# Moving a 31-tap convolution onto VectorE, reordering a mixer's projections, and placing input sums behind evacuations

## The chip, the core and the metric

The kernel runs on one core of a Trainium2 chip. The time is that of one execution on the device, in microseconds (us); three executions of the kernel before were timed. TensorE is called PE, VectorE DVE, ScalarE ACT, GpSimd POOL and SyncE SP, as in the profile.

## The reference, cut to what matters

A trunk of two layers runs over 512 latent tokens (stream x) and 256 context tokens (stream c) of 1024 channels, all in fp32. Each layer is

```
h += 1/2 * gate1 * SwiGLU(mod(RMSNorm(h)))     # FFN, 2816 hidden channels
h +=       gate2 * Mixer(mod(RMSNorm(h)))
h += 1/2 * gate3 * SwiGLU(mod(RMSNorm(h)))
```

The four FFNs are called the first to the fourth (FFN0 to FFN3 in the code's tables). The mixer of layer 0 is a convolution beside a bidirectional gated DeltaNet (GDN); that of layer 1 is a state-space model (S5):

```
h    = a * sigmoid(g)                          # 512 channels, glu of the projection
conv = silu(layer_norm(depthwise31(h) + conv_b))       # 31 taps a channel
qkv  = silu(depthwise5(qkv_raw)); q, k = l2norm(q), l2norm(k)   # 4 heads of 128
y    = concat([conv, gdn(q, k, v, a, beta) * silu(gate)]) @ w_out
```

## The kernel before

**Products.** Activations lie with channels on partitions. Every fp32 product is three fp32r matmuls of high and low parts (L381, L383, L385). A weight tile `raw` comes by DMA on SP; ACT copies its high part `whi` (L163) and DVE, or POOL, subtracts for `wlo` (L164).

**FFN.** The 2816 hidden channels are 22 units of 128. A direct unit is `ua`, `ub` products over 8 row blocks; its evacuation `evac` is silu on ACT, multiply on DVE, high part on ACT, low part on DVE. `NDIR` says how many units of each FFN are direct; the rest are fast units (`up_fast`): seven products of half size, which need sums of the inputs (`fast_sums`, k = 0 to 3, on DVE with two splits on ACT and DVE) and sums of the weights (on POOL). The lists `FP0` to `FP3` say at which point of the FFN each of the four sums is issued: (1, 4) in the middle of the first units' context products, "b2" ahead of unit 2's products, a plain 2 behind unit 2's evacuation. After some units a down projection (`down`, `both`) writes banks d0x, d1x, d0c and so on, and `resid` (L701) adds them to `hT`.

**Second FFN and the S5 build.** While the second FFN runs, a generator `build` makes the matrices of the S5 mixer on DVE, POOL and PE. `with_bg` advances it by `NBG` yields after each step.

**Mixer of layer 0, projections (616 to 872 us).** `MIXORD` lists the steps: a0 the decay inputs, q0 to q5 the projections of two channel blocks each (q0, q1 are q heads, q2, q3 are k heads, q4, q5 are v), g0, g1 the gates, u2, u3 the glu of convolution blocks 2 and 3, k0 to k3 the transposes of a k head to tokens, s0 to s2 small scalar stages. After a q step's products the 5-tap convolution runs (ACT L961, then four DVE operations L963 for each of two blocks), then silu (L969). In the next step, behind its products, `held_back` issues the squares on ACT (L982), which PE sums over channels into `sqn` (L985); L986 takes them to `nrm`. For v the transposes `tt` are copied to `ts` with the factor RINV (L1003).

**Convolution.** `conv31(m, ...)` is a generator, one tap or so a yield. Blocks m = 0, 1 run during the projections: POOL does 10 taps (L862 multiply, L863 add), DVE 21 (L867, L870) and one addition. `conv_taps(n)` issues n yields at the end of a step, by the table `TAPS`. Blocks 2, 3 run beside the GDN: `side_work` loads `hb` from DRAM by SP, then ACT multiplies 16 taps (L873, tile ctt), POOL adds them (L874, tile cvp), DVE does 15 (L870, tile cvs) and an addition (L884).

**GDN (872 to about 1170 us).** `run` goes round its generators (scans, the levels of a triangular inverse, the preparation of the next chunk) and advances each by one yield a round, then `side_work` by one. A level is PE w (L1269), ACT copy (L1270), PE b (L1280), DVE update (L1283); L1231, L1241, L1244, L1250 and L1251 prepare a chunk on DVE or POOL. Each engine works off its instructions in the order of issue.

Of the kernel before, what the change touches and what calls it, by code (L numbers as in the profile page):

```python
# [9 lines left out]
F32 = mybir.dt.float32  # L10
# [4 lines left out]
ALU = mybir.AluOpType  # L15
# [20 lines left out]
TAPU = 8  # L36
# [4 lines left out]
NBG = 5  # L41
S5RD = 3
TSTAT = 1
NDIR = (3, 16, 3, 3)
FP0 = [(1, 4), (1, 7), "b2", 2]
FP1 = [13, 14, "b15", 15]
FP2 = [(1, 4), (1, 7), "b2", 2]
FP3 = [(1, 4), (1, 7), "b2", 2]
# [4 lines left out]
MIXORD = "a0 q0 q1 q2 q3 s0 g0 s1 k0 g1 s2 k1 q4 k2 k3 q5 u2 u3"  # L53
TAPS = (10, 16, 4, 11)
# [5 lines left out]
def trunk_kernel(  # L60
# [468 lines left out]
    def ffn_steps(l, fi, zf, zt, nxt, parts=PARTS, rest=None, fast=0, prep=(), delay=False):  # L529
# [194 lines left out]
        def down(c0, nk, lastpart):  # L724
# [4 lines left out]
            def both(q):  # L729
                def fn(w):  # L730
                    for i in range(0, per, 2):
# [79 lines left out]
    NPOOL, NPOOL2 = TAPS[:2]  # L811
# [15 lines left out]
    def open_mixer():  # L827
# [16 lines left out]
        T["cp"] = p.tile([P, CW], F32, name="cp")  # L844
        T["ct"] = p.tile([P, CW], F32, name="ct")
# [5 lines left out]
    def conv31(m, hb, ca, cp, ct):  # L851

        w = lambda j: cwT[:, j * 4 + m:j * 4 + m + 1]
        n = NPOOL if ct is not None else NPOOL2
        pj = list(range(31 - n, 31))
        cps = cp if isinstance(cp, list) else [(cp, 0, CW)]
        for c_, a, b in cps:
            GP.tensor_scalar(c_, hb[:, pj[0] + a:pj[0] + b], w(pj[0]), par[:, CONVB_O + m:CONVB_O + m + 1], ALU.mult, ALU.add)
        k = 1
        while ct is not None and k < n:  # L860
            for c_, a, b in cps:
                GP.tensor_scalar(ct[:, a:b], hb[:, pj[k] + a:pj[k] + b], w(pj[k]), None, ALU.mult)  # L862
                GP.tensor_tensor(c_, c_, ct[:, a:b], ALU.add)  # L863
            k += 1
        if ct is not None:
            yield
        V.tensor_scalar(ca, hb[:, 0:CW], w(0), None, ALU.mult)  # L867
        yield
        for j in range(1, 31 - n):
            V.scalar_tensor_tensor(ca, hb[:, j:j + CW], w(j), ca, ALU.mult, ALU.add)  # L870
            while k < n and k * (31 - n) < j * n:
                t = tmp.tile([P, SAW], F32, tag="sa", name="ctt")
                SC.activation(t, hb[:, pj[k]:pj[k] + CW], AF.Copy, scale=w(pj[k]))  # L873
                GP.tensor_tensor(cp, cp, t, ALU.add)  # L874
                k += 1
            yield
        while k < n:
            t = tmp.tile([P, SAW], F32, tag="sa", name="ctt")
# [4 lines left out]
        for c_, a, b in cps:  # L883
            V.tensor_tensor(ca[:, a:b], ca[:, a:b], c_, ALU.add)  # L884
# [1417 lines left out]
```

## Time and profile before

| | us |
|---|---|
| three executions, median (lowest to highest) | 2963.92 (2960.92 to 2970.04) |
| the profiled execution | 2967.29 |
| its span | 2965.0 |
| busy PE / DVE / POOL / ACT | 2790.9 / 2066.2 / 1098.0 / 1090.2 |

PE is busy for 94% of the span. The rest is some 170 us of idle stretches, and there are stretches in which PE works at the lower of its clock's two levels (1.2 against 2.4 GHz); a granted clock of 1.00 in a row is the higher level throughout, 0.50 the lower. The page's row of PE in 40 slices shows where both lie: its digits are 8 and 9 but for the first slice and the mixer of layer 0. The views that follow are tables of busy time by stretch, of waits by engine, and of instructions by line. Line numbers are those of the kernel before; the changed kernel's are 1 less up to L840 or so, and 30 less from L920 on.

### The profile page before, as it was taken

The page shows a single profiled execution, that of the slowest core. Times are in us where ns is not written, and L with a number is a line of the kernel's source. Part 1 is how long each engine was busy: PE and PEld are TensorE (multiplying, and loading weights), DVE is VectorE, ACT ScalarE, POOL GpSimd, SP SyncE. Part 2 cuts the span into 40 slices and gives each one's busy share as a digit, 9 for nine tenths or more (in the row PEclk, how much of TensorE's full clock was granted, in tenths as well). Part 3 has the DMA queues.
Part 4 walks back from the last instruction along what each step waited for, and adds up shares of the span by engine and source line. Part 5 has one row for each costly group of instructions (what it writes and reads, how often), then busy time and mean ns, then how long its engine had stood idle before and what let it go on. Part 6 is the DMA issues. An engine that isn't in the chain of part 4 may idle for free. (4 is left out here: it accounts for less than half of the span.)

```text
span 2965.0 us, 49519 instructions
## 1 busy us (share of the span) xinstructions
PE 2790.9 (94%) x19207; PEld 2476.1 (84%) x19207; DVE 2066.2 (70%) x3774; ACT 1090.2 (37%) x2201; POOL 1098.0 (37%) x1182
## 2 busy tenths in 40 slices
PE   7899999998988899998999999999999989899998
PEld 5799999977876668887888899789999977689997
DVE  4676667658857857658665676786777656588887
ACT  4333333334444535432122233443333332344444
POOL 0144343259108723003764043233433300026653
PEclk9899999998897898999999999999999989999999
DMA  6323332121244574322333122122222226533331
GB/s 230 93 85 128 108 120 72 51 86 43 82 147 160 179 253 151 122 63 77 105 119 100 57 62 74 38 84 58 72 71 60 76 67 219 172 100 97 108 100 65
DMA packets 306089, 308.09 MB, mean 104 GB/s; under 512 B 35053, under 2 KB 261513, under 8 KB 299200
## 3 DMA queue, kind: packets, MB, share of 16 engines
q1 hardware_dynamic: 284592, 274.89, 29.8%
q10 hardware_dynamic: 20256, 25.76, 2.6%
q0 software_dynamic: 1008, 4.29, 0.4%
q8 instruction: 152, 2.49, 0.3%
q14 instruction: 81, 0.66, 0.1%
HBM read 279.34 MB, written 25.56 MB: 103 GB/s over the span
## 5 line engine op out<-in xcount | busy, mean ns | idle before, releaser
L164 DVE TENSOR_TENSOR wlo<-raw,whi 128x512 fp32r<-128x512 f32 (+1 forms) x755 | 612.3, 852 | 267.8 <-ACT whi L163 253.5
L163 ACT ACTIVATE whi<-raw 128x512 fp32r<-128x512 f32 (+2 forms) x775 | 450.6, 616 | 628.5 <-PE s L383 196.9
L592 POOL TENSOR_TENSOR raw<-s,raw 128x512 f32<-128x512 f32 x63 | 90.3, 1434 | 409.7 <-DVE wlo L164 394.9
L676 POOL TENSOR_TENSOR gl<-sa,gh 128x384 fp32r<-128x384 f32 (+1 forms) x126 | 130.5, 1056 | 294.8 <-ACT gh L675 294.8
L381 PE MATMUL s<-xnh,whi 128*128 128x384 f32 x704 | 237.1, 337 | 0.0
L385 PE MATMUL s<-xnh,wlo 128*128 128x384 f32 x704 | 236.2, 336 | 0.0
L383 PE MATMUL s<-xnl,whi 128*128 128x384 f32 x704 | 236.0, 335 | 0.0
L381 PE MATMUL s<-xt,whi 128*128 128x384 f32 (+1 forms) x668 | 212.9, 319 | 2.7 <-DVE u L684 2.7
L383 PE MATMUL s<-xt,whi 128*128 128x384 f32 (+1 forms) x668 | 212.9, 319 | 0.0
L385 PE MATMUL s<-xt,wlo 128*128 128x384 f32 (+1 forms) x668 | 212.6, 318 | 0.0
L589 POOL TENSOR_TENSOR s<-raw 128x512 f32<-128x512 f32 x63 | 93.0, 1476 | 300.0 <-DMA raw<-in_ffn_w_dram 300.0
L381 PEld LDWEIGHTS s<-xnh,whi 128*128 128x128 f32 x704 | 132.3, 188 | 7.3 <-issue 5.0
L383 PEld LDWEIGHTS s<-xnl,whi 128*128 128x128 f32 x704 | 132.3, 188 | 0.6
L385 PEld LDWEIGHTS s<-xnh,wlo 128*128 128x128 f32 x704 | 132.3, 188 | 0.0
L381 PEld LDWEIGHTS s<-xt,whi 128*128 128x128 f32 x668 | 127.2, 190 | 2.9 <-ACT whi L163 2.9
L383 PEld LDWEIGHTS s<-xt,whi 128*128 128x128 f32 x668 | 127.1, 190 | 0.0
L385 PEld LDWEIGHTS s<-xt,wlo 128*128 128x128 f32 x668 | 127.1, 190 | 0.0
L595 POOL TENSOR_TENSOR raw<-raw 128x512 f32<-128x512 f32 x63 | 101.2, 1606 | 6.3 <-DVE wlo L164 6.3
L164 POOL TENSOR_TENSOR wlo<-raw,whi 128x512 fp32r<-128x512 f32 x20 | 28.8, 1472 | 193.9 <-ACT whi L163 193.9
L164 POOL TENSOR_TENSOR wlo<-s,whi 128x512 fp32r<-128x512 f32 x63 | 86.8, 1378 | 30.2 <-ACT whi L163 27.6
L383 PE MATMUL pf<-xnl,whi 128*128 128x512 f32 (+1 forms) x256 | 89.5, 349 | 8.7 <-DVE xnl L343 8.5
L591 POOL TENSOR_TENSOR raw<-raw 128x512 f32<-128x512 f32 x63 | 92.2, 1464 | 4.9
(786 smaller groups left out, 8418.8 us busy)
## 6 DMA issues: line engine op xcount, KB each, us to landing
raw<-in_ffn_w_dram SPq DMA_DIRECT2D x176, 512.0 KB
raw<-in_w_mod_dram SPq DMA_DIRECT2D x64, 1024.0 KB
raw<-in_ffn_w_dram SPq DMA_DIRECT2D x32, 1024.0 KB
raw<-in_ffn_w_dram SPq DMA_DIRECT2D x16, 768.0 KB
raw<-in_w_mod_dram SPq DMA_DIRECT2D x16, 512.0 KB
raw<-in_e_w_in_dram SPq DMA_DIRECT2D x8, 1024.0 KB
raw<-in_e_w_out_dram SPq DMA_DIRECT2D x8, 1024.0 KB
CAD<-C ACTq DMA_DIRECT2D x4, 1152.0 KB
```

Of the source, the lines that this page charges most:

```text
L163: SC.activation(hi, src, AF.Copy)
L164: (GP if j.slow or c in j.gp else V).tensor_tensor(lo, src, hi.bitcast(F32), ALU.subtract)
L381: mm(ps, wh, xh, start=first, stop=False)
L383: mm(ps, wh, xl, start=False, stop=False)
L385: mm(ps, wl, xh, start=False, stop=last)
L589: tt(job.s1, q[2], q[3], ALU.add)
L591: tt(q[2], q[0], q[2], ALU.subtract)
L592: tt(q[0], job.s1, q[0], ALU.subtract)
L595: tt(q[1], q[1], q[0], ALU.subtract)
L676: GP.tensor_tensor(gl[:, gslot, s], sa[:, s], gh[:, gslot, s].bitcast(F32), ALU.subtract)
```

## The change

It has three parts. **The sums of the FFNs:** in the first, third and fourth FFN sum 1 goes from the middle of the first units' products to behind their evacuation ("e"), sum 2 from ahead of unit 2 to behind its evacuation, sum 3 from there to the start of the first down projection ("d0", a new point). In the second FFN two more units are direct (18 for 16), the sums move along by two units, and `build` is advanced by 4 yields a step, not 5. **The convolution:** all 31 taps run on DVE; the bias goes into its first operation; beside the GDN two taps are issued a round. The loads of `hb` there go by POOL's and ACT's queues, with 4 and 3 rounds between load and first tap for 2 and 2. **The order of the projections:** `MIXORD` takes the k heads first, their transposes early, and spreads the gates between them; `TAPS` gives 3 yields to a q step, 13 to a gate, 8, 6 and 6 to u2, u3 and a0, and in u2 and u3 they are issued ahead of the products.

```diff
@@ -33,25 +33,24 @@
 LANE = (0, 3)
 MORD = "t t t M t t t c L X c c H c"
 FINP = (1, 1)
-TAPU = 8
 NLAST = 6
 STG = 2
 AFT = 5
 NG = 3
-NBG = 5
+NBG = 4
 S5RD = 3
 TSTAT = 1
-NDIR = (3, 16, 3, 3)
-FP0 = [(1, 4), (1, 7), "b2", 2]
-FP1 = [13, 14, "b15", 15]
-FP2 = [(1, 4), (1, 7), "b2", 2]
-FP3 = [(1, 4), (1, 7), "b2", 2]
+NDIR = (3, 18, 3, 3)
+FP0 = [(1, 4), "e", 2, "d0"]
+FP1 = [15, 16, "b17", 17]
+FP2 = [(1, 4), "e", 2, "d0"]
+FP3 = [(1, 4), "e", 2, "d0"]
 SLOW = (1, 1, 1)
 FPARTS = [3, 2, 2, 2, 2, 2, 2, 2, 2, 3]
 FGP = ("s1",)
 NH = 256
-MIXORD = "a0 q0 q1 q2 q3 s0 g0 s1 k0 g1 s2 k1 q4 k2 k3 q5 u2 u3"
-TAPS = (10, 16, 4, 11)
+MIXORD = "a0 q2 g0 q3 k0 q0 g1 k1 q1 s0 s1 q4 s2 k2 q5 k3 u2 u3"
+TAPS = (3, 13, 8, 6, 6)
 SPREAD = (1, 0.7, 0, 1.6)
 MODS0 = (6, 1)
 
@@ -728,6 +727,8 @@
 
             def both(q):
                 def fn(w):
+                    if c0 + q == 0:
+                        fast_prep("d0")
                     for i in range(0, per, 2):
                         bk = banks([f"d{i}", f"d{i + 1}"], zs)
                         early = q == 0 and i == 0 and (not delay or c0 == 0)
@@ -808,7 +809,6 @@
     dram = ctx.enter_context(tc.tile_pool(name="dram", bufs=1, space=bass.MemoryType.DRAM))
     HW = 918
     CW = 888
-    NPOOL, NPOOL2 = TAPS[:2]
     hD = dram.tile([2, P, HW], F32, name="hD")
     cD = dram.tile([4, P, CW], F32, name="cD")
     sgD = dram.tile([4, P, NT], F32, name="sgD")
@@ -841,47 +841,20 @@
         SC.dma_start(T["tri"], k_mask[:, 0].rearrange("d p f -> p d f"))
         T["hb"] = [p.tile([P, HW], F32, name=f"hb{i}") for i in range(2)]
         T["ca"] = p.tile([P, CW], F32, name="ca")
-        T["cp"] = p.tile([P, CW], F32, name="cp")
-        T["ct"] = p.tile([P, CW], F32, name="ct")
         for i, h in enumerate(T["hb"]):
             GP.memset(h, 0.0)
             GP.dma_start(hD[i], h)
         T["convq"] = []
 
-    def conv31(m, hb, ca, cp, ct):
+    def conv31(m, hb, ca, per=1):
 
         w = lambda j: cwT[:, j * 4 + m:j * 4 + m + 1]
-        n = NPOOL if ct is not None else NPOOL2
-        pj = list(range(31 - n, 31))
-        cps = cp if isinstance(cp, list) else [(cp, 0, CW)]
-        for c_, a, b in cps:
-            GP.tensor_scalar(c_, hb[:, pj[0] + a:pj[0] + b], w(pj[0]), par[:, CONVB_O + m:CONVB_O + m + 1], ALU.mult, ALU.add)
-        k = 1
-        while ct is not None and k < n:
-            for c_, a, b in cps:
-                GP.tensor_scalar(ct[:, a:b], hb[:, pj[k] + a:pj[k] + b], w(pj[k]), None, ALU.mult)
-                GP.tensor_tensor(c_, c_, ct[:, a:b], ALU.add)
-            k += 1
-        if ct is not None:
-            yield
-        V.tensor_scalar(ca, hb[:, 0:CW], w(0), None, ALU.mult)
+        V.tensor_scalar(ca, hb[:, 0:CW], w(0), par[:, CONVB_O + m:CONVB_O + m + 1], ALU.mult, ALU.add)
         yield
-        for j in range(1, 31 - n):
+        for j in range(1, 31):
             V.scalar_tensor_tensor(ca, hb[:, j:j + CW], w(j), ca, ALU.mult, ALU.add)
-            while k < n and k * (31 - n) < j * n:
-                t = tmp.tile([P, SAW], F32, tag="sa", name="ctt")
-                SC.activation(t, hb[:, pj[k]:pj[k] + CW], AF.Copy, scale=w(pj[k]))
-                GP.tensor_tensor(cp, cp, t, ALU.add)
-                k += 1
-            yield
-        while k < n:
-            t = tmp.tile([P, SAW], F32, tag="sa", name="ctt")
-            SC.activation(t, hb[:, pj[k]:pj[k] + CW], AF.Copy, scale=w(pj[k]))
-            GP.tensor_tensor(cp, cp, t, ALU.add)
-            k += 1
-            yield
-        for c_, a, b in cps:
-            V.tensor_tensor(ca[:, a:b], ca[:, a:b], c_, ALU.add)
+            if j % per == 0:
+                yield
         nc.sync.dma_start(cD[m], ca)
         yield
 
@@ -920,13 +893,11 @@
             bc = project_first(ws, "c", True)
             for m in range(2):
                 glu_evac(m, "c", *bc[2 * m:2 * m + 2])
-                cp = T["cp"] if m == 0 else [(tmp.tile([P, 512], F32, tag="sq", name="cq")[:, :b - a], a, b) for a, b in ((0, 444), (444, CW))]
-                T["convq"].append((m, conv31(m, T["hb"][m], T["ca"], cp, T["ct"])))
-            for _, g in T["convq"]:
-                next(g)
+                T["convq"].append((m, conv31(m, T["hb"][m], T["ca"])))
 
         def glu(m):
             def fn(w):
+                conv_taps(TAPS[m])
                 bk = project([(lambda a: lambda k: w.at(a, k))(a) for a in range(2)], ("x", "c"))
                 held_back()
                 sa = tmp.tile([P, SAW], F32, tag="sa", name="gl")[:, :NT]
@@ -937,7 +908,6 @@
                 nc.sync.dma_start(bass.AP(tensor=hD.tensor, offset=hD[m - 2, 0:1, 15:16].offset, ap=[[HW, P], [79, 8], [1, 64]]),
                                   sa[:, XS].rearrange("p (r w) -> p r w", w=64))
                 nc.sync.dma_start(hD[m - 2, :, 647:903], sa[:, CS])
-                conv_taps(TAPU)
             return step(fn, pair_job(W_in, m * P, 512 + m * P, P, KD))
 
         def qkv(q):
@@ -972,7 +942,7 @@
                         T["sqq"].append(t)
                     if t >= 8:
                         T["vq"].append((t - 8, cv))
-                conv_taps(TAPS[2], tick=tick)
+                conv_taps(TAPS[0], tick=tick)
             return step(fn, cols_job(W_in, 1024 + q * 256, 256, KD))
 
         def held_back():
@@ -1013,7 +983,7 @@
                     SC.activation(sa[:, XS], bk["x"][i], AF.Silu)
                     SC.activation(sa[:, CS], bk["c"][i], AF.Silu)
                     nc.sync.dma_start(sgD[2 * q + i], sa[:, :NT])
-                conv_taps(TAPS[3], tick=tick)
+                conv_taps(TAPS[1], tick=tick)
             return step(fn, cols_job(W_in, 2560 + q * 256, 256, KD))
 
         def ab_fn(w):
@@ -1029,6 +999,7 @@
                 V.tensor_copy(T["abt"], pt[:, :96].rearrange("p (c f) -> p c f", c=6))
             T["abq"].append(tok)
             T["chain"] = chain()
+            conv_taps(TAPS[4])
 
         def ab(_):
             return step(ab_fn, cols_job(W_in, 3072, 16, KD))
@@ -1173,7 +1144,6 @@
         WM = [w[:, h * 128:h * 128 + 128] for w in (ring("whi"),) for h in range(4)]
         cvs = [wkp.tile([P, n], F32, name=f"cvs{n}") for n in (HW, CW)]
         WK = [[ring("wlo") for _ in range(4)] for _ in range(2)]
-        cvp = p.tile([P, CW], F32, name="cvp")
         cst, sc, qk, small = T["cst"], T["scl"], T["qk"], T["small"]
         seen = set()
 
@@ -1384,7 +1354,7 @@
                 yield
         done, fin = [], []
 
-        bg = side_work(cvs, cvp)
+        bg = side_work(cvs)
 
         def run(gens, late, after):
             n = 0
@@ -1449,7 +1419,7 @@
             head_out("x", h, range(4), T["sgx"][h])
         close_pool("mxO")
 
-    def side_work(cvs, cp):
+    def side_work(cvs):
 
         def load(m, src=None):
             t = tmp.tile([P, SAW], F32, tag="sa", name="lnc")
@@ -1470,15 +1440,15 @@
                 t, nxt = nxt, load(m + 1, src) if m < 3 else None
                 yield from fn(m, t)
         hb, ca = cvs
-        nc.sync.dma_start(hb, hD[0])
-        yield
-        yield
+        GP.dma_start(hb, hD[0])
+        for _ in range(4):
+            yield
         for m in (2, 3):
-            yield from conv31(m, hb, ca, cp, None)
+            yield from conv31(m, hb, ca, 2)
             if m == 2:
-                nc.sync.dma_start(hb, hD[1])
-                yield
-                yield
+                SC.dma_start(hb, hD[1])
+                for _ in range(3):
+                    yield
 
         def add(m, t):
             if m == 0:

```

ACT in the first FFN, behind unit 2's products: sa and gh are an evacuation, xt, acc and rst the splits of a sum, mod the product that rtmod copies. Before:

```order
L548 ACTIVATE gh<-sa 128x256
L375 ACTIVATE xt<-xs_885 128x2x384
L375 ACTIVATE rst<-xs_886 128x384
L163 ACTIVATE whi_897<-raw_760 128x384
L163 ACTIVATE whi_901<-raw_760 128x384
L163 ACTIVATE whi_905<-raw_760 128x384
L163 ACTIVATE whi_909<-raw_760 128x384
L449 COPY rtmod_927<-mod_731 128x512
```

and now:

```order
L547 ACTIVATE gh<-sa 128x256
L374 ACTIVATE xt<-xs_872 128x2x384
L374 ACTIVATE acc<-xs_873 128x384
L162 ACTIVATE whi_884<-raw_760 128x384
L162 ACTIVATE whi_888<-raw_760 128x384
L162 ACTIVATE whi_892<-raw_760 128x384
L162 ACTIVATE whi_896<-raw_760 128x384
L448 COPY rtmod_914<-mod_731 128x512
L374 ACTIVATE xt<-xs_928 128x2x384
```

The splits ahead of the copy of mod are those of sum 2, and those of sum 3 stand behind it.

DVE in the projections, behind the small convolution of the first head: L963 (now L933) is that convolution, L870 (L855) a tap, small the scalar stages, cr the next head's padding. Before:

```order
L1063 TENSOR_SCALAR small<-small 128x48
L870 SCALAR_TENSOR_TENSOR ca<-hb_5637,cwT,ca 128x888
L1065 RECIPROCAL small<-small 128x48
L870 SCALAR_TENSOR_TENSOR ca<-hb_5637,cwT,ca 128x888
L1067 TENSOR_TENSOR small<-small 128x48
L870 SCALAR_TENSOR_TENSOR ca<-hb_5637,cwT,ca 128x888
L1069 TENSOR_TENSOR small<-small 128x48
L986 TENSOR_SCALAR nrm<-sqn 128x6 x2
L951 MEMSET cr_6205 128x2 x3
```

and now:

```order
L1014 SCALAR_TENSOR_TENSOR small<-small 128x48
L855 SCALAR_TENSOR_TENSOR ca<-hb_5637,cwT,ca 128x888
L1034 TENSOR_SCALAR small<-small 128x48
L855 SCALAR_TENSOR_TENSOR ca<-hb_5637,cwT,ca 128x888
L1036 RECIPROCAL small<-small 128x48
L855 SCALAR_TENSOR_TENSOR ca<-hb_5637,cwT,ca 128x888
L1038 TENSOR_TENSOR small<-small 128x48
L956 TENSOR_SCALAR nrm<-sqn 128x6 x2
L855 SCALAR_TENSOR_TENSOR ca<-hb_5637,cwT,ca 128x888
L1040 TENSOR_TENSOR small<-small 128x48
```

A gate's step follows, with 13 taps and no padding of a next head.

DVE beside the GDN, convolution block 2: cvs is the block's sum. Before:

```order
L870 SCALAR_TENSOR_TENSOR cvs_7621<-cvs_7620,cwT,cvs_7621 128x888
L1283 TENSOR_TENSOR wk<-wk,b 128x2x8x8 x4
L1250 TENSOR_TENSOR V_7609<-wk,lev 128x128
L1251 TENSOR_TENSOR V_7609<-eye,V_7609 128x128
L870 SCALAR_TENSOR_TENSOR cvs_7621<-cvs_7620,cwT,cvs_7621 128x888
L1250 TENSOR_TENSOR V_7613<-wk,lev 128x128
L1251 TENSOR_TENSOR V_7613<-eye,V_7613 128x128
L870 SCALAR_TENSOR_TENSOR cvs_7621<-cvs_7620,cwT,cvs_7621 128x888
```

and now:

```order
L855 SCALAR_TENSOR_TENSOR cvs_7577<-cvs_7576,cwT,cvs_7577 128x888 x2
L1253 TENSOR_TENSOR wk<-wk,b 128x2x8x8 x4
L1220 TENSOR_TENSOR V_7565<-wk,lev 128x128
L1221 TENSOR_TENSOR V_7565<-eye,V_7565 128x128
L855 SCALAR_TENSOR_TENSOR cvs_7577<-cvs_7576,cwT,cvs_7577 128x888 x2
L1220 TENSOR_TENSOR V_7569<-wk,lev 128x128
L1221 TENSOR_TENSOR V_7569<-eye,V_7569 128x128
L855 SCALAR_TENSOR_TENSOR cvs_7577<-cvs_7576,cwT,cvs_7577 128x888 x2
```

Two taps stand where one stood.

## Rows read from the trace of the kernel before

**Rows 1.** Windows, busy us of PE, PEld, DVE, ACT, POOL; PEclk, DMA, GB/s.

```profile
616.00:872.00 256.00, 237.20 (x1329) 206.23 (x1328) 171.52 (x272) 100.82 (x194) 116.11 (x66) 0.91 0.26 79
872.00:1030.00 158.00, 129.12 (x1887) 96.53 (x1886) 119.54 (x255) 76.18 (x198) 121.49 (x127) 0.78 0.51 177
1262.00:1850.00 588.00, 562.32 (x3334) 504.87 (x3333) 397.86 (x878) 159.22 (x296) 230.01 (x428) 0.98 0.27 83
```

**Rows 2.** Waits of PE, 0 to 616: total us, times, longest us.

```profile
PE modt L465 <- ACT rtmod L449: 13.0, 1, 13.0
```

**Rows 3.** Timeline of ACT, 100 to 118: start, length, [idle before <- releaser].

```profile
111.05 0.84 ACT L375 ACTIVATE xt<-xs 128x768 fp32r<-128x768 f32 x1 [5.44 <-DVE xs L642]
...
113.86 0.56 ACT L449 COPY rtmod<-mod 128x512 f32<-128x512 f32 x1
```

**Rows 4.** Waits of PE, 616 to 872 (projections of the mixer).

```profile
PE sqn L985 <- ACT sq L982: 14.6, 3, 7.6
PE pj0x L381 <- ACT ts L1003: 3.2, 2, 2.7
```

**Rows 5.** Groups by line, 616 to 872: count, busy us, mean ns of one.

```profile
L870 DVE SCALAR_TENSOR_TENSOR ca<-hb,cwT,ca 128x888 f32<-128x888 f32 x40 | 51.0, 1276 | 0.9
...
L164 DVE TENSOR_TENSOR wlo<-raw,whi 128x512 fp32r<-128x512 f32 x40 | 31.6, 850 | 22.2 <-ACT whi L163 22.1
...
L963 DVE SCALAR_TENSOR_TENSOR acc<-cr,par,acc 128x770 f32<-128x770 f32 x24 | 30.8, 1283 | 0.3
```

**Rows 6.** Line 870 alone, tile of the GDN: ns min/median/max of one.

```profile
L870 DVE SCALAR_TENSOR_TENSOR cvs<-cvs,cwT,cvs x28: 1127/1190/2976, 888.9 to 1016.6; 128x888 f32<-128x888 f32 x28
```

**Rows 7.** Line 963 alone, one of its two tiles: ns min/median/max.

```profile
L963 DVE SCALAR_TENSOR_TENSOR acc<-cr,par,acc x24: 1012/1022/1971, 673.1 to 846.4; 128x770 f32<-128x770 f32 x24
```

**Rows 8.** Two stretches of the second FFN: one direct unit, then two fast ones.

```profile
1612.72:1629.53 16.81, 16.81 (x97) 14.87 (x97) 4.46 (x9) 4.14 (x8) 0.00 (x0) 1.00 0.38 116
1716.43:1745.59 29.16, 29.16 (x170) 29.16 (x168) 26.20 (x36) 13.84 (x26) 12.48 (x9) 1.00 0.37 109
```

**Rows 9.** Waits of PE, 872 to 1030 (GDN while the convolution runs beside it).

```profile
PE vt L1257 <- DVE wk L1251: 9.1, 5, 5.6
PE vt L1257 <- POOL wk L1251: 5.7, 2, 4.9
PE vt L1257 <- POOL V L1251: 4.8, 2, 3.7
...
PE w L1269 <- DVE V L1283: 2.9, 1, 2.9
```

**Rows 10.** Windows: the two convolutions beside the GDN.

```profile
888.00:947.00 59.00, 48.71 (x680) 35.11 (x681) 45.47 (x73) 25.73 (x60) 51.33 (x49) 0.67 0.34 117
958.00:1019.00 61.00, 49.51 (x716) 36.63 (x714) 47.58 (x106) 28.82 (x71) 52.40 (x48) 0.80 0.52 186
```

**Rows 11.** Groups by line, 872 to 1030.

```profile
L870 DVE SCALAR_TENSOR_TENSOR cvs<-cvs,cwT,cvs 128x888 f32<-128x888 f32 x28 | 43.5, 1554 | 0.3
...
L1231 DVE SCALAR_TENSOR_TENSOR wk<-wk,cst,neg 128x128 f32<-128x128 f32 x24 | 19.2, 857 | 0.0
```

**Rows 12.** The same group of line 1231 later, 1030 to 1172.

```profile
L1231 DVE SCALAR_TENSOR_TENSOR wk<-wk,cst,neg 128x128 f32<-128x128 f32 x16 | 5.6, 420 | 0.0
```

**Rows 13.** Waits of DVE, 872 to 1030.

```profile
DVE cvs L867 <- DMA cvs<-hD: 7.3, 2, 5.1
```

**Rows 14.** Waits of PE, 1262 to 1850 (second FFN).

```profile
PE d4x L381 <- DVE hT L701: 14.2, 5, 3.7
PE uax L385 <- DVE wlo L164: 5.0, 2, 3.4
PE pq L1780 <- POOL Q L1730: 4.5, 1, 4.5
```

**Rows 15.** Waits of PE, 1850 to 2375 (third FFN).

```profile
PE d0x L381 <- ACT gh L548: 5.5, 1, 5.5
```


## The prediction

> **What bounds the kernel now.** PE does: it is busy in all but a few per cent of every stretch of the FFNs. So an edit counts only where PE waits, or where waiting has left it at the lower clock. I read first the table of busy time by stretch [rows 1], to see where PE is short of full: the projections of the mixer (237 of 256 us busy, granted clock 0.91) and the GDN (129 of 158, clock 0.78); the second FFN loses 26 of 588. Then the waits of PE in each stretch, which name the tile that was late and its engine [rows 2, 4, 9, 14, 15], and last the instructions behind those names.
>
> **Sums of the first FFN.** PE waits 13.0 us, once, for a copy called rtmod [rows 2]. On ACT that copy starts at 113.86, behind the splits of sum 3; these had ACT idle for 5.44 us while DVE worked at the sum, and took 1.35 themselves [rows 3]. In the new order only three sums stand ahead of the copy, not four, so it is issued earlier by one sum: 5.44 + 1.35 = 6.8 us at most, less if the weights copied in front of it come late. I take **6 us** (3 to 7). The other 6 or 7 us of the wait stay. Sum 3 then runs while PE does the down products, which hide it.
>
> **Projections.** Of the 17.8 us that PE waits here, 14.6 are three waits for squares [rows 4]. A head's products take PE 16.8 us (the same 96 matmuls as a direct unit's, [rows 8]). DVE's work for a head is eight small-convolution steps, four weight parts and four taps: 8 x 1.27 + 4 x 0.85 + 4 x 1.28 = 18.7 us [rows 5], so in a row of four heads it falls behind by 2 us a head. POOL is the reason that the first and last of these are so long: a tap takes 1.13 at least [rows 6], a small step 1.02 in the median and 1.97 at most [rows 7], and POOL is busy for 116 us there [rows 1]. With POOL's taps gone and three yields a head, it is 8 x 1.02 + 3.4 + 3 x 1.13 = 15.0 us. A gate's step costs 13 x 1.13 + 3.4 = 18.1 against 16.8; two of them lose 2.6, which the slack of 1.8 in each of six heads covers. If that cover is gone, 2.6 is lost. I walked the new order of ACT and PE with these durations: the squares behind table loads keep about 5 of the 14.6, and the waits behind ts, 3.2 now, become about 5 since RINV is ready later and the v heads end the row. So 17.8 goes to 10: 8 us. A clock of 0.91 means 46 us at the lower level, half of it lost; with the waits halved I take 3 of these 23. **11 us** (3 to 18). DVE's sum there hardly moves: 20 more taps are 23 us, the shorter steps and taps give back about as much.
>
> **GDN.** Here the unknown is largest. What goes: 5.7 + 4.8 us of waits for POOL [rows 9], which is busy for 51 and 52 us in the two stretches of 59 and 61 in which the blocks are convolved, where DVE has 45.5 and 47.6 [rows 10]. What comes: 60 taps for 28 on DVE. By the minimum of 1.127 [rows 6], 60 taps are 67.6 us; the 28 took 43.5, at 1.554 each [rows 11]. The 24 operations of L1231 took 0.857 each, and 0.420 later, with less POOL work about [rows 11, 12]: 10.5 us go, some 7 of them in the two stretches. So DVE has 93.1 - 43.5 + 67.6 - 7 = 110 us in the same 120: 92% busy, after 78%. Were it to work without a break, the stretches would shrink by 10; if it fills no more than 78% again, they grow to 141. A tap is always ready, which speaks for a full queue; that two stand together and hold up each update by 1.13 us speaks against it. I take 95%, 116 us: 4 less. The loads are a second item: DVE stood 7.3 us for them, twice [rows 13], with the updates behind it that PE then waited for (2.9 for w, and 2 or so of the 9.1 for vt [rows 9]). With one and two more rounds, of about 3.5 us, they have landed: 4 or 5. Together **8 us** (-16 to +17). POOL's and ACT's queues, which the loads are moved to, hold nothing there that waits on them; ACT loses 32 products.
>
> The Trainium skill, Perfetto Trace Analysis, "Optimizing Scalar/DVE Operations", says that where DVE is saturated, moving work off it to ScalarE or GpSimd may help, though perhaps not to GpSimd, with which it shares a read port. The first half speaks against this change, which moves ACT's and POOL's taps to the fuller engine; by it the GDN's term is a loss and the first rival below holds. The trace so far agrees more with the second half, since the same operation takes 0.857 beside POOL's work and 0.420 with less.
>
> **Second FFN.** Three groups of waits [rows 14]. uax waits 5.0 us for a weight's low part, behind bursts of 41 and 50 build operations on DVE in the order of before; there are 21 and 40 now: 4.4 of it goes. pq waits 4.5 us for POOL; its products stand later in PE's order now: 4.5. d4x waits 14.2 us for resid, in five waits; three of 3.7 stand behind bursts of 30, now of 18 to 26: half of those 11.2, 5.6. The clock is 0.98 over the 588 us [rows 1], so some 23 us run at the lower level, half of which is loss; as the waits go, I take 4 back. Against that stand two more direct units: 16.81 us for one direct, 29.16 for two fast ones, so 2.23 more each, 4.4 [rows 8]. Together 4.4 + 4.5 + 5.6 + 4 - 4.4 = **14 us** (6 to 19; at the low end the bursts still delay the resids and the clock gives nothing).
>
> **Sums of the third and fourth FFN.** In the third, PE waits 5.5 us for gh of unit 2 at the start of the down products [rows 15]; sum 2 stood ahead of that evacuation and stands behind it now. A sum, 5.4 us as in the first FFN, leaves the path: **5 us** (3 to 6). Next in line is bank d0x, which comes free behind sum 3 and its resid; by the trace that is about when PE wants it again. The fourth FFN has no such wait: 0 (-1 to +2).
>
> **Sum.** 6 + 5 + 14 + 11 + 8 = 44 us. The profiled execution took 2967.3 (span 2965.0), so 2923; it lies 3.4 above the median of the runs, so **2920**.
>
> **Rivals.**
> *DVE becomes the bound of the mixer (slower).* If taps keep 1.28 and 1.55 us without POOL beside them, because what lengthened them was another thing, 32 more are 49.7 us in the GDN: 119.5 + 49.7 = 169 us of DVE work in a stretch of 158 [rows 1], which at 90% busy takes 188, a loss of 30. In the projections a gate's step would be 20 us and a head's 17.4 against 16.8: a loss of 5. Against the FFNs' 25 that is 10 slower: 2974. It decides from a mean tap of about 1.4 us in the GDN. For it: DVE is already the releaser of PE's longest wait there. Against it: the minimum and median of 1.13 and 1.19 [rows 6].
> *Waits only move.* Squares, ts copies and DVE's pairs of taps bring back in the mixer what POOL gives free; the FFNs' 25 remain: 2939. For it: ACT's table loads and the v heads at the end. Against it: the DVE sum of a head falls below PE's.
> *The clock comes back too.* In the GDN the clock of 0.78 means 70 us at the lower level; if PE has its operands early enough to stay at the higher one for a third of that, 12 more are won there and 8 more in the projections: 2900. For it: 1.00 wherever PE is fed. Against it: PE's work in the GDN is small matmuls in a chain with ACT and DVE.
> *The second FFN doesn't do what it says.* The bursts still stand ahead of the down products, so the resids may come as late as before, and the two direct units cost 4.4: 14 + 4 less, 2938.
>
> **How the numbers follow.** The forecast has 0.56 (2905 to 2935 by its own bounds), the clock 0.16, waits that only move 0.14, the second FFN 0.07, DVE as the bound 0.07. The range of 2895 to 2950 leaves out half of the clock's case and most of the last one, under 0.2 in all. A change of 0.3% (9 us) is about what a measurement of this kernel can tell from none. Faster by more than that: all of the first two and nearly all of the next two, 0.88; within it 0.06, where losses of the GDN eat the rest; slower 0.06.
>
> **What would show it.** In the profile after: the wait of modt at about 7 us and none for gh in the third FFN; no wait of uax for a weight and none of pq in the second, and d4x under 10; a mean tap near 1.15 in both stages and L1231 near 0.45; POOL nearly idle from 616 to 1030; squares at 5 us and ts at 5; DVE over 90% busy in the convolved stretch of the GDN. The prediction is wrong if taps stay above 1.3, if the GDN up to the last tap is longer than 158 us, or if the FFNs give less than 15 together.

## Result and profile after

| | us |
|---|---|
| before, median of four executions (lowest to highest) | 2963.98 (2960.92 to 2970.04) |
| after, median of four (lowest to highest) | 2898.80 (2895.00 to 2900.06) |
| after, profiled execution / its span | 2895.0 / 2893.2 |

The ratio to before is 0.9775, with a 95% interval of 0.9757 to 0.9794: 65 us less, where 44 were forecast. Both profiles can be cut at the same instructions of PE: the first product behind the last wait of each of the first three FFNs (t0x), the start of the GDN (growbc) and of the second FFN's norm (rrow). From PE's records and the granted clock of each stretch:

| stage | length before / after | idle of PE | at the lower clock |
|---|---|---|---|
| first FFN | 571.8 / 564.3 | 30.9 / 24.6 | 30.7 / 23.9 |
| projections (to growbc) | 300.2 / 281.3 | 24.6 / 14.2 | 44.4 / 23.9 |
| GDN and output projection | 362.9 / 344.7 | 42.3 / 38.3 | 102.4 / 58.0 |
| second FFN | 602.4 / 580.0 | 26.2 / 8.6 | 23.9 / 3.4 |
| third FFN | 530.7 / 524.3 | 11.4 / 7.6 | 6.8 / 0.0 |
| the rest | 597.0 / 598.6 | 30.6 / 29.1 | 44.4 / 47.8 |

So 7.5 + 18.9 + 18.2 + 22.4 + 6.4 - 1.6 = 71.8 us lie between the two profiled spans. (After's profiled execution is the shortest of its four and before's is above its median; hence 72 here and 65 between the medians. Its GDN is also near the short end of what the same code takes in the runs below, 344.5 to 353.4 us with a median of 347.8; against that median the stage gained 15, not 18.) Windows of the profile after, as [rows 1] and [rows 10] of before; the columns are the same, and the third is the stretch in which the two convolutions run beside the GDN:

```profile
608.00:846.00 238.00, 229.52 (x1332) 199.06 (x1333) 163.72 (x291) 101.04 (x195) 7.51 (x10) 0.95 0.28 85
846.00:1004.00 158.00, 134.29 (x2180) 101.33 (x2179) 139.27 (x327) 56.83 (x200) 65.65 (x117) 0.91 0.61 210
856.00:987.00 131.00, 109.75 (x1876) 83.45 (x1876) 122.83 (x268) 43.40 (x157) 54.74 (x85) 0.92 0.56 200
1218.00:1784.00 566.00, 557.92 (x3356) 499.27 (x3356) 381.28 (x866) 154.46 (x287) 213.60 (x414) 1.00 0.29 86
```

POOL is down to 7.5 us in the projections and the clock is up in every row: 0.91 to 0.95, 0.78 to 0.91, 0.98 to 1.00. DVE is busy for 94% of the convolved stretch. The waits of PE after, in the order first FFN, projections, second FFN, third FFN (as [rows 2, 4, 14, 15]; a wait that is missing has gone):

```profile
PE modt L464 <- ACT rtmod L448: 6.3, 1, 6.3
...
PE sqn L955 <- ACT sq L952: 3.5, 2, 2.1
PE pj0x L380 <- ACT ts L973: 3.0, 2, 2.6
...
PE d4x L380 <- DVE hT L700: 6.1, 4, 2.3
...
PE d0x L380 <- DVE hT L700: 1.5, 1, 1.5
```

And in the GDN while the convolution runs beside it, 846 to 1004 (as [rows 9]):

```profile
PE w L1239 <- DVE wk L1253: 6.4, 2, 3.2
...
PE vt L1227 <- DVE wk L1221: 2.6, 3, 2.2
...
PE vt L1227 <- POOL wk L1221: 2.3, 1, 2.3
```

The waits of vt for POOL fell from 10.5 us to 2.3 and those for DVE from 9.1 to 2.6, but a new one came: w waits 6.4 us for DVE's updates.

And the instructions that DVE runs there: a tap of the GDN's convolutions and the operation of line 1201 (1231 before, [rows 11]), then a small step of the projections alone (as [rows 7]):

```profile
L855 DVE SCALAR_TENSOR_TENSOR cvs<-cvs,cwT,cvs 128x888 f32<-128x888 f32 x60 | 71.5, 1192 | 1.4
L1201 DVE SCALAR_TENSOR_TENSOR wk<-wk,cst,neg 128x128 f32<-128x128 f32 x24 | 8.4, 411 | 0.0
...
L933 DVE SCALAR_TENSOR_TENSOR acc<-cr,par,acc x24: 1015/1021/1025, 663.8 to 816.0; 128x770 f32<-128x770 f32 x24
```

A tap fell from 1.55 to 1.19 us and line 1201 from 0.86 to 0.41; of the small step not one takes longer than 1.025, where 1.97 was seen before.

### The profile page after: what moved, and what is told of

Its sections match the earlier page's. It is cut to its first block, busy times and chain, and to the rows that moved or that the text cites. A ratio compares the mean times of both kernels' runs of the same rounds, so it can differ in the third digit from the quotient of the medians.

```text
span 2893.2 us, 49426 instructions
## 1 busy us (share of the span) xinstructions
PE 2762.3 (95%) x19231; PEld 2452.4 (85%) x19231; DVE 2044.2 (71%) x3807; ACT 1058.7 (37%) x2164; POOL 909.5 (31%) x1080
## 3 DMA queue, kind: packets, MB, share of 16 engines
q1 hardware_dynamic: 284304, 273.95, 30.6%
## 5 line engine op out<-in xcount | busy, mean ns | idle before, releaser
L163 DVE TENSOR_TENSOR wlo<-raw,whi 128x512 fp32r<-128x512 f32 (+1 forms) x751 | 602.1, 843 | 253.9 <-ACT whi L162 246.0
L380 PE MATMUL s<-xnh,whi 128*128 128x384 f32 x672 | 226.2, 337 | 0.0
L384 PE MATMUL s<-xnh,wlo 128*128 128x384 f32 x672 | 225.2, 335 | 0.0
L382 PE MATMUL s<-xnl,whi 128*128 128x384 f32 x672 | 225.0, 335 | 0.0
L380 PE MATMUL s<-xt,whi 128*128 128x384 f32 (+1 forms) x648 | 206.0, 318 | 3.9 <-DVE u L683 3.9
L384 PE MATMUL s<-xt,wlo 128*128 128x384 f32 (+1 forms) x648 | 205.8, 318 | 0.7 <-DVE wlo L163 0.7
L382 PE MATMUL s<-xt,whi 128*128 128x384 f32 (+1 forms) x648 | 205.9, 318 | 0.0
L380 PEld LDWEIGHTS s<-xnh,whi 128*128 128x128 f32 x672 | 126.2, 188 | 7.3 <-issue 5.0
L380 PEld LDWEIGHTS s<-xt,whi 128*128 128x128 f32 x648 | 123.4, 190 | 4.2 <-ACT whi L162 4.2
L382 PEld LDWEIGHTS s<-xt,whi 128*128 128x128 f32 x648 | 123.3, 190 | 0.0
L594 POOL TENSOR_TENSOR raw<-raw 128x512 f32<-128x512 f32 x61 | 98.7, 1617 | 4.6 <-DVE wlo L163 4.6
L380 PE MATMUL pf<-xnh,whi 128*128 128x512 f32 (+1 forms) x256 | 88.5, 346 | 3.2 <-ACT xnh L339 2.6
```

The lines of the kernel that those rows point to most:

```text
L163: (GP if j.slow or c in j.gp else V).tensor_tensor(lo, src, hi.bitcast(F32), ALU.subtract)
L380: mm(ps, wh, xh, start=first, stop=False)
L382: mm(ps, wh, xl, start=False, stop=False)
L384: mm(ps, wl, xh, start=False, stop=last)
L594: tt(q[1], q[1], q[0], ALU.subtract)
```

## Experiments

Each run is the changed kernel with the edit shown, compared with 2898.8. The changed kernel was timed in the first set of executions only, where before had 2964.0; in the later sets, beside which these runs stand, the median of before is 2963.8 to 2967.0. So a few us between two runs are read with the intervals of their ratios to before, given in brackets, and with the lengths of stages.

### The FFNs' sums back

```diff
-FP0 = [(1, 4), "e", 2, "d0"]
+FP0 = [(1, 4), (1, 7), "b2", 2]
...
-FP2 = [(1, 4), "e", 2, "d0"]
+FP2 = [(1, 4), (1, 7), "b2", 2]
```

(The fourth FFN's list goes back in the same way.)

> The changed kernel with the input sums of the first, third and fourth FFN at their old places (all else as changed). Theory: the sums are worth what the two traces show in those FFNs, 7.5 us in the first and 6.4 in the third, and the three parts of the change add up, so this run takes 2898.8 + 14 = 2913 us, with a wait of modt of 13 us and one of d0x of 5.5 again. Rival: the first FFN's wait only moved because other work moved with it, then the run stays within 4 us of 2898.8.

Measured: 2908.9 (ratio to before 0.9815, 0.9798 to 0.9831). The two waits are back as they were:

```profile
PE modt L464 <- ACT rtmod L448: 12.8, 1, 12.8
...
PE d0x L380 <- ACT gh L547: 5.5, 1, 5.5
```

The first FFN takes 572.2 again and the third 531.1, 7.9 and 6.8 more than after. The medians are 10 apart, not 14; single executions of one kernel differ by 5 to 10 us, so the stage lengths are the better measure. In these two stages the sums act independently of the rest.

### The second FFN: units and yields

```diff
-NBG = 4
+NBG = 5
-NDIR = (3, 18, 3, 3)
+NDIR = (3, 16, 3, 3)
-FP1 = [15, 16, "b17", 17]
+FP1 = [13, 14, "b15", 15]
```

> The changed kernel with the second FFN as before (16 direct units, 5 build yields a step, its sums one unit pair earlier). Theory: that FFN is worth the 22.5 us by which its stretch got shorter, so 2921 us, with waits of 5.0 (uax), 4.5 (pq) and 14 (d4x) and five stretches at the lower clock again. Rival: part of the 22.5 came from the order in which the stages ahead of it left the engines; then 2910 or less.

Measured: 2926.7 (0.9870, 0.9855 to 0.9885), 28 more. The waits are uax 5.0, pq 4.5 and d4x 14.2 again, and 30.7 us of that FFN run at the lower clock. Its stretch is 24.8 longer than after's. The rest lies in the GDN, whose code is the same (353.4 us here; its spread is told below).

Two runs take one half each. With 16 direct units and their sums, but 4 yields (`NDIR` and `FP1` back, `NBG` as changed):

> The changed kernel with 16 direct units and the sums at their old places in the second FFN, but 4 build yields a step. Theory: the shorter bursts alone take the waits away (uax 5.0, pq 4.5 and 8 of d4x's 14), and the two more direct units only cost their 4.4 us: 2894, with gaps of 9 us and under 10 us at the lower clock in that FFN. Rival: the build lasts longer at 4 a step, and without the two more direct units it still runs when the fast units' weight sums need POOL; then waits of pq or of the fast units' products appear and the run takes 2900 or more.

With 18 direct units and 5 yields (`NBG = 5` alone):

> The changed kernel with 5 build yields a step (18 direct units as changed). Theory: the bursts of 30 to 50 operations stand ahead of the weights and the resids again, so uax and d4x wait 12 us more together and the clock falls behind each of these waits (some 10 us of loss): 2917 to 2922. Rival: the position of the bursts, not their length, made the waits; then 2899 to 2905.

Measured: 2915.6 (0.9843, 0.9819 to 0.9866) and 2925.6 (0.9864, 0.9849 to 0.9879). Waits of PE in that FFN, first with 4 yields and 16 units, then with 5 and 18:

```profile
PE pm L1791 <- DVE C L1700: 9.4, 1, 9.4
PE d4x L380 <- DVE hT L700: 7.0, 3, 3.7
PE pq L1750 <- POOL Q L1700: 2.8, 1, 2.8
```

```profile
PE d4x L380 <- DVE hT L700: 14.3, 5, 3.8
PE uax L384 <- DVE wlo L163: 5.0, 2, 3.3
PE pq L1750 <- POOL Q L1700: 3.9, 1, 3.9
```

The second run went as its theory said, even above it: the bursts make the waits. In the first the theory fell and its rival held. Shorter bursts take uax's wait and half of d4x's away, but the build is not done in time, and a product pm waits 9.4 us for it. So the two direct units (with the sums' places that go with them), which I had booked only as a cost of 4.4 us, are what makes room for the slower build. Of the 28 us, 4 yields alone keep 11, and two more direct units alone 1; by the length of the second FFN (604.8 us in the first run, 594.6 and 606.8 here) it is 10 and none of 25.

### The GDN's convolutions on ACT, POOL and DVE again

```diff
-            yield from conv31(m, hb, ca, 2)
+            yield from conv31_shared(m, hb, ca, cvp)
```

(`conv31_shared` is the old form for blocks 2 and 3: 15 taps on DVE, 16 multiplied by ACT and added by POOL, one DVE tap a round. The loads stay on the new queues with the longer lead.)

> The changed kernel, but the two convolution blocks beside the GDN are shared out as before (16 taps multiplied by ACT and added by POOL, 15 on DVE, one tap a round); the loads stay on the new queues with their longer lead. Theory: POOL's work beside DVE lengthens taps (back to 1.5 us from 1.18) and line 1201's operations (back to 0.8 from 0.41), PE waits for POOL and falls to a granted clock of 0.8, and 13 of the GDN's 17 us are lost: 2912. Rival (DVE is the bound in either form, and the gain came from the loads): 2897 to 2902.

Measured: 2913.1 (0.9820, 0.9801 to 0.9840), 14 more. Rows of this run, the convolved stretch and the two groups on DVE:

```profile
857.00:993.00 136.00, 111.76 (x1820) 84.42 (x1820) 103.96 (x219) 67.91 (x179) 113.49 (x113) 0.83 0.55 193
```

```profile
L870 DVE SCALAR_TENSOR_TENSOR cvs<-cvs,cwT,cvs 128x888 f32<-128x888 f32 x28 | 45.8, 1636 | 0.3
...
L1227 DVE SCALAR_TENSOR_TENSOR wk<-wk,cst,neg 128x128 f32<-128x128 f32 x24 | 13.6, 626 | 0.0
```

The taps are at 1.64 us, PE's clock at 0.83, and the GDN with the output projection takes 361.4 us: 16.7 more than after and only 1.5 less than before. The loss lies clear of the 344.5 to 353.4 us that this stage takes in the eight profiles with the changed kernel's code there. The 1.5 us are less than this spread: of the longer lead of the loads, for which I had booked 4 or 5 us, no gain at the end can be told from it. The first step of the scan comes 74.1 us behind growbc before, 62.5 in this run and 57.2 after, but the last one comes at 306.3, 305.7 and 287.5. It may be that what the loads give at first is spent by the three rounds that the side work is longer; no run has the loads' new lead and queues alone undone, so that is not shown.

### The old order of the projections

```diff
-MIXORD = "a0 q2 g0 q3 k0 q0 g1 k1 q1 s0 s1 q4 s2 k2 q5 k3 u2 u3"
-TAPS = (3, 13, 8, 6, 6)
+MIXORD = "a0 q0 q1 q2 q3 s0 g0 s1 k0 g1 s2 k1 q4 k2 k3 q5 u2 u3"
+TAPS = (4, 11, 8, 8, 2)
```

> The changed kernel with the old order of the projections (q heads first, k heads and gates late), all 31 taps on DVE, 4 yields a q step and 11 a gate. Theory: the projections got shorter because POOL's taps no longer lengthen DVE's operations; the order matters less: of the 19 us gained there 13 stay, 2905, with squares late by about 7 us in sum. Rival: the order did it, because four heads in a row are too much for DVE either way (8 x 1.02 + 3.4 + 4 x 1.13 = 16.1 us a head against 16.8, so by the sum it should not be): 2912 to 2918 and 14 us of waits for squares.

Measured: 2904.2 (0.9794, 0.9779 to 0.9809). The projections take 282.0 us, against 281.3 after: neither order was worth anything there, which goes further than the theory. The 5 us lie behind them. I first put them down to the spread of the GDN, and a last run, with the old order and sum 2 late (see below), was to tell:

> The changed kernel with the old order of the projections and sum 2 of the first FFN late, both at once. The run with the old order alone was 5 us above the changed kernel, though its projections were as long; its GDN, whose code is the same, was longer. Theory: that was the GDN's spread from execution to execution, the order is worth nothing, and this run takes 2893 to 2897 with projections of 282 us. Rival: the order is worth 5 us in what follows it; then 2899 or more, and the GDN and output projection at 350 us or more again.

Measured: 2901.7 (0.9788, 0.9771 to 0.9805), where the same kernel with the new order took 2894.6. By its own numbers the theory fell, though the intervals of the two runs overlap. DVE around the start of the GDN, which is at 848.1 in the run with the old order and 845.6 after, first the old order:

```profile
828.72 14.12 DVE L855 SCALAR_TENSOR_TENSOR ca<-hb,cwT,ca 128x888 f32<-128x888 f32 x12
842.75 0.68 DVE L907 TENSOR_TENSOR gl<-pj0x,gl 128x512 f32<-128x512 f32 x1
843.35 0.42 DVE L907 TENSOR_TENSOR gl<-pj0c,gl 128x256 f32<-128x256 f32 x1
843.69 8.30 DVE L855 SCALAR_TENSOR_TENSOR ca<-hb,cwT,ca 128x888 f32<-128x888 f32 x7
...
852.96 2.15 DVE L1201 SCALAR_TENSOR_TENSOR wk<-growbc,cst,neg 128x128 f32<-128x128 f32 x8
```

and then after:

```profile
836.75 5.85 DVE L855 SCALAR_TENSOR_TENSOR ca<-hb,cwT,ca 128x888 f32<-128x888 f32 x5
842.52 0.68 DVE L907 TENSOR_TENSOR gl<-pj0x,gl 128x512 f32<-128x512 f32 x1
846.25 0.42 DVE L907 TENSOR_TENSOR gl<-pj0c,gl 128x256 f32<-128x256 f32 x1 [3.04 <-ACT gl L906]
...
846.72 2.16 DVE L1201 SCALAR_TENSOR_TENSOR wk<-growbc,cst,neg 128x128 f32<-128x128 f32 x8
```

With the old order and this tap table seven taps are still to do when the last glu's products are ready, and the GDN's first operations on DVE start 4.9 us behind growbc, not 1.1. The first tap of block 2 comes 15.6 and 15.4 us behind growbc in these two runs, and 11.1 in the eight profiles with the new order that have the same code there; the first step of the scan comes at 62.9 and 61.9, and at 57.0 to 60.3 in the eight. So there is a lag of some 4 or 5 us at the seam to the GDN. That it lasts is not shown: the last step comes at 294.4 and 294.6, within the eight's 287.4 to 297.4, and so does the stage, with 351.9 and 350.2 us within 344.5 to 353.4. Nor is the lag one that the change took away, for the kernel before, with the old order but other taps and another table, has none; growbc is at 872.0 there:

```profile
873.08 2.15 DVE L1231 SCALAR_TENSOR_TENSOR wk<-growbc,cst,neg 128x128 f32<-128x128 f32 x8
```

So the lag belongs to the tap table that these two runs have, and the old order by itself is not shown to cost anything.

### Useless work for POOL in the projections

```diff
+                GP.tensor_scalar(cp, hb[:, 0:CW], cwT[:, m:m + 1], None, ALU.mult)
+                for k in range(1, 10):
+                    GP.tensor_scalar(ct, hb[:, k:k + CW], cwT[:, k * 4 + m:k * 4 + m + 1], None, ALU.mult)
+                    GP.tensor_tensor(cp, cp, ct, ALU.add)
```

> The changed kernel with POOL given useless work in the projections: for each of the first two convolution blocks one multiplication and nine pairs of a multiplication and an addition, 128x888, as before the change, into a tile that nobody reads. No instruction waits for it, so any loss is what POOL's work does to others. Theory: the small convolution's steps (line 933, 1.02 us) rise to a mean of 1.25 and the taps from 1.13 to 1.25, squares come late by 10 to 15 us again, and the run takes 2908 to 2915. Rival: POOL beside DVE costs little, the order and the shorter list per head did it: 2897 to 2902.

Measured: 2929.5 (0.9875, 0.9860 to 0.9889), 31 more, nearly all of it in the projections (311.7 us for 281.3). Nobody waits for this work, so this is what POOL does to DVE's instructions alone, and it is twice what I had expected, though the instructions grew no more than I had said: a tap to 1.26 us in the mean, a small step only to 1.13. A tap, and a scalar stage of 128x8 (line 1031 here), with the shortest, median and longest of each in ns:

```profile
L857 DVE SCALAR_TENSOR_TENSOR ca<-hb,cwT,ca x60: 1039/1144/2957, 642.7 to 872.7; 128x888 f32<-128x888 f32 x60
```

```profile
L1031 DVE TENSOR_TENSOR small<-abt,adt x6: 153/156/2073, 666.6 to 668.9; 128x8 f32<-128x8 f32 x6
```

Of the 60 taps 52 are as short as ever and eight are longer by 0.6 to 1.8 us; an operation on eight columns of 0.16 us took 2.07 and ended at 668.68, just behind an addition of POOL at 668.65. So it isn't that both share a rate: the one is held up by an instruction of the other. DVE is then late with the small steps, and squares wait 20.8 us. The variant that only writes:

```diff
+                for k in range(28):
+                    GP.memset(cp, 0.0)
+                    GP.memset(ct, 0.0)
```

> As the run with POOL's useless work, but with 112 memsets of 128x888 in place of it: POOL is busy and writes, but reads nothing. If it is POOL's reading that lengthens DVE's operations with two inputs, taps and line 933 stay at 1.13 and 1.02 and the projections at 281 us; if any work of POOL does, they rise as in that run.

Measured: 2951.6, one execution, with projections of 330.8 us. Neither answer was right. DVE there, from the timeline:

```profile
637.42 2.50 DVE L163 TENSOR_TENSOR wlo<-raw,whi 128x512 fp32r<-128x512 f32 x4
639.84 66.11 DVE L854 TENSOR_SCALAR ca<-hb,cwT,par 128x888 f32<-128x888 f32 x1
705.98 4.68 DVE L857 SCALAR_TENSOR_TENSOR ca<-hb,cwT,ca 128x888 f32<-128x888 f32 x4
```

The memsets run from 617.8 to 705.5. The taps with two inputs all follow, from 706.0 on, so they say nothing of them. What ran beside the memsets is the split of the weights, which has two inputs too; first that line in the run whose POOL reads, then beside the memsets:

```profile
L163 DVE TENSOR_TENSOR wlo<-raw,whi x41: 283/684/2596, 631.1 to 843.5; 128x512 fp32r<-128x512 f32 x40, 128x128 fp32r<-128x128 f32 x1
```

```profile
L163 DVE TENSOR_TENSOR wlo<-raw,whi x8: 281/686/693, 632.1 to 639.2; 128x512 fp32r<-128x512 f32 x7, 128x128 fp32r<-128x128 f32 x1
```

These eight are as fast as without POOL (0.694 us at most after). But the first tap, which has one input and takes 0.74 us by itself, stood for 66.11 us, until the last memset had ended (705.5), and PE stood for 46 us behind it.

### One tap a round, and three

```diff
-            yield from conv31(m, hb, ca, 2)
+            yield from conv31(m, hb, ca, 1)
```

> The changed kernel with one tap a round beside the GDN, not two. The convolutions then need some 30 rounds more than the GDN has, and what is left of the side work runs alone at its end. Theory (DVE's total is what matters while taps run, and pairs hold up nothing of weight): the round gets shorter while taps run, but the tail of 25 to 30 us at the end more than takes it back, 2905 to 2925. Rival (pairs of taps hold up DVE's updates by 1.13 us a round and PE behind them): the stage wins 15 or more before the tail, and the run ends at 2890 to 2900.

And with 3 in that place:

> The changed kernel with three taps a round beside the GDN. Theory: a round with three taps (3.4 us) and 1.4 us of other work is longer than PE's and ACT's part, so PE waits for updates more in 21 rounds and less in the ten that get free of taps: 2898 to 2906. Rival (pairs already hold PE up by their length): 2910 or more, with DVE named as the releaser of 20 us of PE's waits between 846 and 960.

Measured: 2922.5 (0.9860, 0.9834 to 0.9887) and 2919.9 (0.9844, 0.9813 to 0.9875), both over 20 more. With one tap the rounds are quicker: the scan's first five steps come 51, 100, 146, 193 and 235 us behind growbc, for 57, 109, 160, 205 and 250 after. But the sixth comes at 318 for 288, since what is left of the side work stands alone at the end: PE waits 18.2 us for the layer norm's sums, 2.4 after. So the theory had the total and the rival the quicker rounds. With three taps the first two steps come at 68 and 134, and the clock in their stretch is 0.79:

```profile
857.00:968.00 111.00, 83.78 (x1304) 62.37 (x1298) 101.81 (x188) 25.52 (x91) 43.66 (x64) 0.79 0.49 172
```

The rival held there: DVE is named for 27 us of PE's waits between 846 and 960. The wait of w for DVE's updates (tile wk at L1253), new with the change at 6.4 us, is gone from 846 to 1004 with one tap a round and is 7.8 with three. So the second tap of a pair costs a little (6 us by the first step), the third much (11 more), and of the three two is the best.

### Sum 2 of the first FFN late

```diff
-FP0 = [(1, 4), "e", 2, "d0"]
+FP0 = [(1, 4), "e", "d0", "d0"]
```

> The changed kernel with sum 2 of the first FFN too put at the start of the first down projection, ahead of sum 3. If the rest of modt's wait (6.25 us) is that sum, the wait falls to 1 us and the run to 2893; d0x's second use comes some 14 us after its first by the third FFN's rows, and two sums of 5.3 and its resid are done by then. Rival: the resids come late behind two sums and PE waits for d0x instead: 2898 to 2902.

Measured: 2894.6 (2891.9 to 2898.0; ratio to before 0.9767, 0.9741 to 0.9792). The wait of modt falls from 6.3 to 2.3 us and that FFN from 564.3 to 560.8. That is a better kernel than the changed one by some 4 us; the two intervals overlap, so the trace shows the gain and the times only agree with it.

## Why the prediction was right, and where it was short

The time lies in the range (2895 to 2950), near its low end, and the direction was right. By its steps:

- **Waits.** Booked as gone were 6 + 5 in the first and third FFN, 14.5 in the second, 8 in the projections and 8 in the GDN, together 41.5. PE's idle time fell by 6.3 + 3.8 + 17.6 + 10.4 + 4.0 + 1.5 = 43.6 by the table above. Single items moved: d4x lost 8.1 us, not 5.6; squares kept 3.5 us, not 5; ts stayed at 3.0 instead of rising to 5; the GDN's idle time lost 4, not 8, since w's new wait for pairs of taps took back 6.4 of what POOL had given free. That the sums agree to 2 us is in part luck.
- **The clock** is the term that was mis-sized. I booked 4 us for the second FFN, 3 for the projections and nothing for the GDN. The time at the lower level fell by 20.5, 20.5 and 44.4 us there, and by 6.8 each in the first and third FFN. Half of that is the gain where PE is fed: 10 and 10 in the first two, so 14 became 22.4 (17.6 + 10.2 - 4.4 = 23.4 by the parts) and 11 became 18.9 (10.4 + 10.2 = 20.6). In the GDN idle time fell by only 4 and the stage by 18.2; the other 14.2 are busy time of PE. There half is too much, for PE's products are small: a product of w takes 0.218 us at the higher level and 0.311 at the lower (rows below), 1.4 times as long. As an estimate from these two, 44.4 us less at the lower level give back 44.4 x (1 - 0.218 / 0.311) = 13.3. Why the clock stayed up there with only 4 us less of idle time, no run parts; the longest wait fell from 5.6 us to 3.2. This is the rival "the clock comes back too" (2900), which had 0.16; the second FFN, where I did not expect it, did the same.
- **It could have been read.** Before, with each of the five larger waits in the second FFN (3.4 to 4.5 us) come 3.4 or 6.8 us at the lower level, 23.9 in all: a wait of 3.7 us cost 5 to 7. One of d4x's waits ends at 1474.3; the stretch ahead of it, and that around its end:

```profile
1440.00:1470.00 30.00, 30.00 (x190) 27.12 (x189) 22.07 (x60) 9.35 (x18) 21.88 (x60) 1.00 0.26 82
1473.20:1480.00 6.80, 5.68 (x14) 4.53 (x15) 6.08 (x13) 0.00 (x0) 6.33 (x10) 0.50 0.57 154
```

I had the row of the whole FFN (0.98 of 588 us) and took a third of it, for no reason that a row gave. The products of w in the GDN before, at 0.50 (921 to 943.5) and at 1.00 (1042 to 1080):

```profile
L1269 PE MATMUL w<-wk x32: 311/311/366, 930.1 to 931.7; 64*64 64x64 f32 x32
```

```profile
L1269 PE MATMUL w<-V,wk x160: 218/218/268, 1043.9 to 1077.4; 64*64 64x64 f32 x160
```

- **DVE in the GDN** went as worked out: taps at 1.19, line 1201 at 0.41, 94% busy for the 95% taken. The two stretches of taps, 59 and 61 us in the working, took 50 and 65 (856.7 to 906.6, 921.5 to 986.6): 5 less, where 4 were booked. The sign that POOL would be nearly idle from 616 to 1030 failed in its second part: it is busy for 7.5 us in the projections, but still for 65.7 of the GDN's 158, with the GDN's own operations.
- **Loads**: 4 or 5 us booked. DVE's waits for them are gone, but the pause between the two blocks grew from 10 us to 15, and in the end no gain is told from the spread (the run with the shared convolution).
- **Order of the projections**: the working credited it, beside POOL's absence, with the shorter list per head. With the old order the projections are as short (282.0 us for 281.3), so none of their gain needs the new one; POOL's work alone puts 30 us back.
- **Direct units**: booked as a price only; the run with 16 shows that without them the build is late.

The rule of the Trainium skill that I weighed (Perfetto Trace Analysis, "Optimizing Scalar/DVE Operations": with DVE saturated, offloading may help) did not decide here: with 16 of 31 taps taken off a DVE that is otherwise 94% busy the kernel is 14 us slower. The runs agree with its second half, that GpSimd may be no help since it shares a port with DVE: a tap took 1.64 us beside POOL's share and 1.19 without.

What stays open: the loads beside the GDN, and the ten taps a block that POOL had done in the projections, were not put back by themselves; the run with useless work stands in for the latter. And single stages of identical code differ between executions. The GDN with its output projection took 344.5 to 353.4 us in the eight profiles with the new order, with 58 to 92 us at the lower clock; why the clock falls in one execution and not in another, no run here shows.

## What to carry to other kernels

Price a wait of PE with the time at the lower clock behind it; in the four stages where PE was otherwise fed, the idle time that went, with half of the lower-clock time that went with it, is 1.5 to 2 times the idle time alone. Before work is moved to a third engine to relieve DVE, compare the mean of DVE's operations beside that engine's work with their minimum: if they differ, the relief is paid back, here with interest. And when a change pairs an obvious price with a gain (more direct units, fewer yields), undo each half alone before calling one of them a cost.

## What the runs showed of the hardware

POOL's operations can hold DVE's up, and which ones depends on the operands. DVE's splits with two inputs in SBUF ran at full speed beside POOL's memsets (0.693 us at most, 0.694 after). Beside POOL's operations that read, some of DVE's with two inputs waited up to 1.9 us (the split up to 2.60 us, a tap up to 2.96, one operation of 0.16 up to 2.07). DVE's operation with one input, 0.74 us alone, waited once through some 66 us of memsets that followed one another without a break. The Trainium skill, SBUF — State Buffer, "SBUF: two separate sides", says that the port pair that DVE and GpSimd share is an exclusive lock held for a whole instruction, taken by a DVE operation in a two-port mode, or by one with two SBUF inputs and then only against a GpSimd operation that reads SBUF. The runs agree where there are two inputs; whether the operation with one input ran in a two-port mode, no run here shows. That an engine can be kept waiting for many instructions of the other in a row, these 66 us show beyond it.

A small product of TensorE is lengthened by less than the ratio of the two clock levels: the records of a 64x64 product show 0.311 us at the lower and 0.218 at the higher.
